# A diffusion-transformer layer on one core: the adaLN vectors move from VectorE to TensorE, and the sums of the projection from GpSimd to VectorE

## Chip, cores and metric

The kernel runs on one core of a Trainium2 chip. The metric is the device time of one execution in microseconds (us); lower is better. Everything is fp32 at the edges; inputs and weights are read from HBM, the output is written there.

## What is computed

One layer over 1,024 latent tokens of width 1,024, with 256 context tokens. The part that the change touches:

```python
sh1, sc1, gt1, sh2, sc2, gt2 = split(silu(c) @ w_mod + b_mod, 6)   # adaLN; w_mod is 1024 x 6144
h = rmsnorm(x, g_pre1) * (1 + sc1) + sh1
q, k, v, f, g_a, g_f = split(h @ w_in)                             # the projection
... attention, Fourier mixing, gated merge, w_out ...
x = x + gt1 * rmsnorm(y, g_post1)
h2 = rmsnorm(x, g_pre2) * (1 + sc2) + sh2
x = x + gt2 * rmsnorm(conv_ffn(h2), g_post2)
```

`sh1` and `sc1` are needed before the first projection matmul. `gt1`, `sh2`, `sc2` and `gt2` are needed only after the merge, far behind the projection.

## The kernel before

**Products.** A fp32 product is three fp32r matmuls (`mm3`, L83 to L87): high part by high, high by low, low by high. Each operand is split by `split`: a copy on ScalarE gives the high part (`hP_g`, `T2a0`), a subtraction on VectorE (L68) the low part (`lP_g`, `T2a1`).

**Items.** The projection is a Strassen product (Winograd's form, function `wino`). Thirteen pairs of 128-column blocks of `w_in` (`g0` to `g7` for the gates, `kv`, `q0`, `q2`, `f0`, `f2`) have seven products each, `P1` to `P7`: 91 items. An item is 12 matmuls of 128x512 into one PSUM bank `X`, `Y` or `Z`. The weights' side needs four sums of two inputs for each pair, `S1` to `S4` (`do_add`; tiles `S_g`, `A_g`); in the kernel before GpSimd makes them. The activations' side is made once: `B11`, `B21`, `B22` and the sums `T1` to `T4n`, cut from the tiles `hr` (`hraw`), which are the normed, transposed and modulated tokens.

**Norm stage.** The first 17 items (0 to 16: `P1`, `P2`, `P5`, `P6`, `P7` of `g0` to `g2`, then `P4` and `P3` of `g0`) are mixed with the loading, squaring, scaling, turning (`turn`, `ptx`) and modulating of the tokens, in an order written out by hand under `tc.manual_schedule()`. An engine takes its instructions in just that order. The first two adaLN vectors are made there on TensorE: `mod_rows` multiplies 32-column groups of the vector (`sv32`) with stages of `w_mod` (`ws`, tiles of the pool `ha`), `mod_copy`, `mod_turn` and `mod_vec` bring the result into columns.

**Projection.** Items 17 to 90 run in `run(17, NI - 5)` and a few lines behind it. For each item `lead` prepares what comes some items later; hooks set by `at(k)` run ahead of item k. The eight other adaLN groups (512 columns each) are made by such hooks: `adaln_load` loads 128x512 pieces of `w_mod` into `wm` tiles (six buffers), `adaln_step` adds one piece, times an element of the vector, to a running sum on VectorE (L723, L725), and `gate_rows` or `col_vec` sums over partitions with a matmul of ones (`pg`, L686, and `pc`, L699). `gate_rows` also loads two rows (`bt`, `gp`), combines them with the result and stores it for later. Behind the projection come the key, value and context pieces and the attention.

**Queues.** All DMAs named here are issued by SP in program order, and each waits for the one eight places ahead of it to land.

Of the kernel before, what the change touches and what calls it, by code (L numbers as in the profile page):

```python
# [16 lines left out]
P = 128  # L17
# [23 lines left out]
def block_kernel(ctx: ExitStack, tc: tile.TileContext, t: dict, out: bass.AP, dbg: dict):  # L41
# [28 lines left out]
    def add(out, a, b, eng=None):  # L70
        return tt(out, a, b, ALU.add, eng)

    def sub(out, a, b, eng=None):
        return tt(out, a, b, ALU.subtract, eng)
# [130 lines left out]
                    items.append((j, p))  # L205
        return items

    def wino(pairs, items, psf, hooks, slots=False):

        st = [dict() for _ in pairs]

        def ready(j):

# [25 lines left out]
        def do_add(j, o):  # L241

            d, nm, w = st[j], pairs[j][2], pairs[j][4] * P
            if o in d:
                return
            if o == "S1":
                d[o] = s(f"{o}_{nm}")[:, :w]
                add(d[o], d["A21"], d["A22"], nc.gpsimd)
            elif o == "S3":
                d[o] = d["A21"]  # L250
                sub(d[o], d["A11"], d["A21"], nc.gpsimd)
            elif o == "S2":
                d[o] = d["A11"]
                sub(d[o], d["S1"], d["A11"], nc.gpsimd)
            else:
                d[o] = d["A12"]
                sub(d[o], d["A12"], d["S2"], nc.gpsimd)

        def do_conv(j, p, eng=None):
            if p in st[j]:  # L260
# [417 lines left out]
    def at(k, *fns):  # L678
        hooks.setdefault(k, []).extend(fns)
# [1 line left out]


    def gate_rows(i, h):
        def done(acc):
            pg = ps(f"pg{i}{h}")
            nc.tensor.matmul(pg, ones, acc, start=True, stop=True)  # L686
            bt, gp = s(f"bt{i}{h}"), s(f"gp{i}{h}")
            load(out=bt, in_=t["rows"][2 * i:2 * i + 1, h * 512:(h + 1) * 512].to_broadcast([P, 512]))
            load(out=gp, in_=t["rows"][2 * i + 1:2 * i + 2, h * 512:(h + 1) * 512].to_broadcast([P, 512]))
            add(bt, pg, bt)  # L690
            mul(bt, bt, gp, nc.gpsimd)
            store(out=gt_d[i, :, h * 512:(h + 1) * 512], in_=bt)
        return done

    def col_vec(w, h):
        def done(acc):
            pc = ps(f"pc{w}{h}")
            for k in range(4):
                nc.tensor.matmul(pc[:, k:k + 1], acc[:, k * P:(k + 1) * P], ones[:, 0:1], start=True, stop=True)  # L699
# [9 lines left out]
    groups = []  # L709
    for h in range(2):  # L710
        for c0, done in ((2 * D, gate_rows(0, h)), (3 * D, col_vec(0, h)), (4 * D, col_vec(1, h)), (5 * D, gate_rows(1, h))):
            groups.append((c0 + h * 512, done))
    wmt, accs = {}, {}

    def adaln_load(i):
        g, k = divmod(i, KT)
        wmt[i] = wm_load(k, groups[g][0])

    def adaln_step(i):
        g, k = divmod(i, KT)  # L720
# [6 lines left out]
    def a0(i):  # L727
        return 17 + i * 7 // 8

    for i in range(8 * KT):  # L730
        at(a0(i), lambda i=i: adaln_load(i))
        at(a0(i) + 4, lambda i=i: adaln_step(i))
        if i % KT == KT - 1:
            at(a0(i) + 7, lambda g=i // KT: groups[g][1](accs[g]))
# [106 lines left out]
    c128, alt = [], []  # L841
    for i, k in enumerate((14, 11)):
        at(NI - k, lambda i=i: late_loads(i))
    run, lead, main, pre, conv, sums, mm, evac, after, st = wino(pairs, items, ps, hooks)
    with tc.manual_schedule():
        for tk in range(4):
            x_load(tk)
# [41 lines left out]
        mod_copy(0)  # L889
        mod_turn(0)  # L890
        mod_vec(0)
        for c in (0, 1, 2, 3):
            x_first(c, (0, 1))
        hb_part(hb, "B11", {c: hraw[c, 0] for c in (0, 2, 1, 3)}, 0, 2)
        mod_rows(1, range(8))
        mod_copy(1)
        mod_turn(1)
        mod_vec(1)
        for tk in range(4):
            x_first(tk, (2, 3))  # L900
# [28 lines left out]
        engs = (nc.vector, None, nc.gpsimd, nc.vector)
        b21 = {c: hraw[c, 1] for c in (0, 3, 1, 2)}  # L930
        for c in range(4):
            x_second(c, (0, 1), engs[c])
        mod_vec(3)
        hb_part(hb, "B21", b21, 0, 2, nc.gpsimd)
# [12 lines left out]
        conv(1, "P2")
        x_square(7)
        x_norm(6)
        for tk in (6, 7):  # L950
            x_scale(tk, 0, nc.vector)
        hb_part(hb, "B21", b21, 2, 4)
        for tk in (4, 5):
            x_scale(tk, 1, nc.gpsimd)
        conv(2, "P2")
        mm(4, range(2))
        for tk in (4, 5):
            x_first(tk, range(4))
        mm(3, range(2, 4))
# [11 lines left out]
        for tk in (6, 7):
            x_scale(tk, 1, nc.gpsimd)
        hb_puts(hb, "T1", {c: hraw[c, 0] for c in range(2)})
        t1(2)
        t1(3)
        conv(0, "P5")
        hb_puts(hb, "T1", {c: hraw[c, 0] for c in range(2, 4)})
        for j in range(1, 3):
            sums(j, "S1")
        for j in range(3):  # L980
            evac(j)
        for j in range(3, 6):
            evac(j, True)
        for tk in (4, 5):
            x_first(tk, range(4), 1)
        conv(1, "P5")
        mm(6)
        for tk in (6, 7):
            turn(tk, 1)
        conv(2, "P5")  # L990
        for j in range(7, 9):
            mm(j)
# [10 lines left out]
        for j in range(9, 12):
            mm(j)
        for c in range(4):
            sub(hraw[c + 4, 0], hraw[c + 4, 1], hraw[c + 4, 0], nc.gpsimd)
# [12 lines left out]
        for j in range(12, 15):
            mm(j)  # L1020
# [1040 lines left out]
```

## Time and profile before

| | |
|---|---|
| median of 3 runs | 1392.88 us (1390.83 to 1396.58) |
| profiled execution | 1390.7 us |
| its span, first to last instruction | 1388.9 us, mean granted clock 0.972 |
| TensorE, VectorE, ScalarE, GpSimd busy | 92%, 77%, 49%, 46% of the span |

The profiled execution is 2.2 us under the median, and 1.8 us of it lie outside the span. A matmul's busy time overlaps its neighbour's, so the pace of TensorE is read from the starts of its matmuls, and its idle time from the waits. The granted clock is a share of full speed: 1.00 is 2.4 GHz, 0.50 is 1.2 GHz.

### The profile page before, as it was taken

The numbers are of one execution on the slowest core, as the hardware profiler recorded it, in microseconds if no ns is written. First come the engines' busy times: TensorE is split into PE (matmuls) and PEld (weight loads), VectorE is DVE, ScalarE is ACT, GpSimd is POOL, SyncE is SP. The second block draws the span as 40 slices with busy tenths as digits, with TensorE's granted clock in tenths as the row PEclk, the third lists the DMA queues.
The fourth block names the chain that finished last, engine by engine and source line by source line (L and its number), as shares of the span: only waits on it lengthen the run. The fifth ranks groups of instructions, "written<-read, shape, count | busy, mean of one in ns | idle before, by whom it ended". The sixth has DMA issues, their size and how long they took to land.

```text
span 1388.9 us, 18347 instructions
## 1 busy us (share of the span) xinstructions
PE 1275.4 (92%) x5848; PEld 1031.8 (74%) x5848; DVE 1075.3 (77%) x1714; ACT 676.2 (49%) x1392; POOL 632.1 (46%) x471
## 2 busy tenths in 40 slices
PE   4759989998999999999979999999999988989896
PEld 3548878776878877777757788888888876878774
DVE  4587899988688986644899997666666687796977
ACT  5456334235567675323756554444444454443442
POOL 0483556553243333611586444444344345372754
PEclk9879999999999999999999999999999999999998
DMA  9714766753524344813603465444434559846563
GB/s 306 228 43 131 238 207 229 251 143 116 142 69 134 110 124 122 302 59 106 190 16 99 131 174 143 129 128 111 121 107 126 167 163 290 294 137 223 180 205 122
DMA packets 251125, 219.42 MB, mean 158 GB/s; under 512 B 14972, under 2 KB 204052, under 8 KB 251028
## 3 DMA queue, kind: packets, MB, share of 16 engines
q1 hardware_dynamic: 251028, 218.25, 51.1%
q8 instruction: 46, 0.75, 0.2%
q14 instruction: 51, 0.42, 0.1%
HBM read 159.20 MB, written 58.72 MB: 157 GB/s over the span
## 4 chain that ended last, share of the span: by engine, by line
PE 52%; DVE 23%; DMA 9%; issue 7%; ACT 4%; POOL 3%; SPq 1%; DVEq 0%; POOLq 0%; ACTq 0%
PE X_u L86 5%; PE X_u L87 5%; PE X_u L85 5%; PE Y_u L85 2%; PE Y_u L87 2%; PE Y_u L86 2%; DVE p L1219 2%; DVE pl L68 2%; PE X_d L85 2%; PE X_d L86 2%; PE X_d L87 2%; DMA ws<-in_w_mod 2%; DVE lP_g L68 1%; PE y L85 1%; PE Z_u L86 1%
## 5 line engine op out<-in xcount | busy, mean ns | idle before, releaser
L68 DVE TENSOR_TENSOR lP_u<-A_u,hP_u 128x512 fp32r<-128x512 f32 x132 | 103.8, 795 | 45.5 <-ACT hP_u L299 45.5
L361 ACT COPY snP_u<-X_u 128x512 f32<-128x512 f32 x57 | 33.5, 587 | 140.8 <-PE X_u L87 132.5
L68 POOL TENSOR_TENSOR A_u<-A_u,A_u 128x512 f32<-128x512 f32 x44 | 71.5, 1625 | 36.4 <-DVE lP_u L68 18.2
L1239 POOL TENSOR_SCALAR p<-p,sm 128x640 f32<-128x640 f32 (+1 forms) x64 | 48.3, 775 | 84.3 <-PE pp L1244 39.2
L68 POOL TENSOR_TENSOR yd<-yd,snP_d 128x512 f32<-128x512 f32 x36 | 52.0, 1448 | 72.8 <-ACT snP_d L361 72.8
L68 POOL TENSOR_TENSOR A_u<-S_u,A_u 128x512 f32<-128x512 f32 x22 | 29.5, 1343 | 107.3 <-DVE lP_u L68 107.0
L299 ACT CAST hP_u<-A_u 128x512 fp32r<-128x512 f32 x121 | 74.6, 619 | 0.1
L361 ACT COPY snP_d<-X_d 128x512 f32<-128x512 f32 x48 | 28.1, 585 | 83.2 <-PE X_d L87 81.6
L80 ACT CAST ph<-pp 128x512 fp32r<-128x512 f32 x76 | 44.3, 585 | 23.3 <-PE pp L1244 21.9
L68 DVE TENSOR_TENSOR pl<-pp,ph 128x512 fp32r<-128x512 f32 x76 | 51.7, 681 | 3.2 <-ACT ph L80 2.7
L1233 ACT ACTIVATE p<-p,nm 128x640 f32<-128x640 f32 (+1 forms) x64 | 51.3, 802 | 0.7 <-DVE nm L1226 0.7
L1549 POOL TENSOR_SCALAR z<-xr,ry 128x512 f32<-128x512 f32 x15 | 16.7, 1123 | 75.3 <-DVE ry L68 65.1
L68 DVE TENSOR_TENSOR lP_d<-rP_d,hP_d 128x384 fp32r<-128x384 f32 x48 | 42.3, 882 | 10.8 <-ACT hP_d L299 10.5
L1244 PE MATMUL pp<-ident,p 128*128 128x128 f32 x304 | 47.0, 274 | 3.9 <-DVE pl L68 2.0
L1219 DVE CUSTOM_DVE_ANT_0 p<-ss,mask 128x640 f32<-128x640 f32 (+1 forms) x64 | 49.9, 782 | 0.0
L725 DVE SCALAR_TENSOR_TENSOR acc<-wm,sv,acc 128x512 f32<-128x512 f32 x56 | 49.2, 879 | 0.6
L1244 PEld LDWEIGHTS pp<-ident,p 128*128 128x128 f32 x304 | 37.0, 140 | 13.6 <-POOL p L1239 3.7
L68 POOL TENSOR_TENSOR wd<-wd,wd 128x512 f32<-128x512 f32 x22 | 37.0, 1700 | 20.3 <-DVE dB L68 11.5
L1624 DVE SCALAR_TENSOR_TENSOR tb<-u,vec,tb 128x1024 f32<-128x1024 f32 x22 | 40.2, 1827 | 6.9 <-ACT tb L1621 6.9
L68 DVE TENSOR_TENSOR u<-Y_u,snP_u 128x512 f32<-128x512 f32 x22 | 15.2, 690 | 38.7 <-PE Y_u L87 38.7
L68 DVE TENSOR_TENSOR dB<-wd,dB 128x512 fp32r<-128x512 f32 x33 | 38.8, 1185 | 8.1 <-ACT dB L1695 8.0
L68 DVE TENSOR_TENSOR lP_g<-A_g,hP_g 128x512 fp32r<-128x512 f32 x48 | 40.3, 853 | 4.5 <-ACT hP_g L80 4.4
(893 smaller groups left out, 4719.9 us busy)
## 6 DMA issues: line engine op xcount, KB each, us to landing
A_u<-in_w_up SPq DMA_DIRECT2D x88, 256.0 KB, 3.7
wm<-in_w_mod SPq DMA_DIRECT2D x66, 256.0 KB, 5.3
wd<-in_w_down SPq DMA_DIRECT2D x55, 256.0 KB, 4.1
A_g<-in_w_in SPq DMA_DIRECT2D x32, 256.0 KB, 5.3
ws<-in_w_mod SPq DMA_DIRECT2D x30, 256.0 KB, 6.0
bP_d<-g_d0P SPq DMA_DIRECT2D x56, 128.0 KB, 3.2
x<-in_x SPq DMA_DIRECT2D x16, 256.0 KB, 5.6
sga_d<-c_g SPq DMA_DIRECT2D x16, 256.0 KB, 3.0
```

Source lines behind the costliest of these rows:

```text
L68: return (eng or nc.vector).tensor_tensor(out=out, in0=a, in1=b, op=op)
L80: copy(hi, src)
L85: nc.tensor.matmul(ps, ah, bh, start=start, stop=False, skip_group_check=True)
L86: nc.tensor.matmul(ps, ah, bl, start=False, stop=False, skip_group_check=True)
L87: nc.tensor.matmul(ps, al, bh, start=False, stop=stop, skip_group_check=True)
L299: copy(st[j]["half", p][0], st[j][STA[p]])
L361: copy(d["s" + p], d["X"])
L725: nc.vector.scalar_tensor_tensor(out=accs[g], in0=wmt[i], scalar=sv[:, k:k + 1], in1=accs[g], op0=ALU.mult, op1=ALU.add)
L1219: nc.vector.tensor_tensor_reduce(out=p_, in0=ssc[:, lo:768], in1=self.mk, op0=ALU.add, op1=ALU.max, scale=1.0, scalar=-3.0e38, accum_out=s ...
L1233: nc.scalar.activation(out=self.pt[g], in_=self.pt[g], func=AF.Exp, scale=SCALE, bias=self.m[:, g:g + 1], accum_out=self.sm[:, g:g + 1])
L1239: nc.gpsimd.tensor_scalar(out=self.pt[g], in0=self.pt[g], scalar1=self.sm[:, g:g + 1], scalar2=1.0, op0=ALU.mult, op1=ALU.mult)
L1244: nc.tensor.transpose(pp[:, g * P:(g + 1) * P], self.pt[g][:, j * P:(j + 1) * P], ident)
```

## The change

Three things change together.

1. The eight adaLN groups go to TensorE in 32-column groups, as `mod_rows` does already. `ada_load` loads the eight pieces of a group, `ada_rows` multiplies them in two halves of four matmuls, `ada_copy` copies the bank out on ScalarE, and `ada_done` calls `gate_rows` or `col_vec`, which now use `sel0` and `sel` in place of `ones`. Groups 0 to 5 (both halves of gate 1, shift 2, scale 2) stand in the norm stage's hand order, 0 and 1 with `gate_rows`, 2 to 5 with `col_vec`; groups 6 and 7 (gate 2) are hooks of items 20 to 45.
2. The sums `S1` to `S4` of the projection, the product `bt * gp`, and the two-input and scaling work of the norm stage leave GpSimd for VectorE (the second scalings `x_scale(tk, 1, ...)` and part of `x_second` for ScalarE).
3. The norm stage's hand order is new: whole items in place of halves, `x_second` and `B21` earlier, `T1` in one piece, sums and conversions of `P5` and `P6` item by item.

```diff
-    def wino(pairs, items, psf, hooks, slots=False):
+    def wino(pairs, items, psf, hooks, slots=False, seng=None):
+        seng = seng or nc.gpsimd
-                add(d[o], d["A21"], d["A22"], nc.gpsimd)
+                add(d[o], d["A21"], d["A22"], seng)
...
     def gate_rows(i, h):
-        def done(acc):
+        def done(rows):
             pg = ps(f"pg{i}{h}")
-            nc.tensor.matmul(pg, ones, acc, start=True, stop=True)
+            nc.tensor.matmul(pg, sel0, rows, start=True, stop=True)
             bt, gp = s(f"bt{i}{h}"), s(f"gp{i}{h}")
...
             add(bt, pg, bt)
-            mul(bt, bt, gp, nc.gpsimd)
+            mul(bt, bt, gp)
...
-    def adaln_step(i):
-        g, k = divmod(i, KT)
-        if k == 0:
-            accs[g] = s(f"acc{g}")
-            nc.vector.tensor_scalar_mul(accs[g], wmt[i], sv[:, k:k + 1])
-        else:
-            nc.vector.scalar_tensor_tensor(out=accs[g], in0=wmt[i], scalar=sv[:, k:k + 1], in1=accs[g], op0=ALU.mult, op1=ALU.add)
...
+    def ada_load(g, ks, spare=True):
+
+        for k in ks:
+            if k < 6 and spare:
+                if k % 3 == 0:
+                    st_.append(hbp.tile([P, 3, 512], F, tag="ha", name=f"wa{g}{k}", bufs=10))
+                wmt[g, k] = st_[-1][:, k % 3, :]
+                load(out=wmt[g, k], in_=w_mod[k * P:(k + 1) * P, groups[g][0]:groups[g][0] + 512])
+            else:
+                wmt[g, k] = wm_load(k, groups[g][0])
+
+    def ada_rows(g, half):
+        if half == 0:
+            rowp[g] = ps(f"ar{g}")
+        for k in range(half * 4, half * 4 + 4):
+            o = k % 4 * 32
+            nc.tensor.matmul(rowp[g][o:o + 32, :], sv32[:, k, :], wmt[g, k], start=k < 4, stop=k >= 4, skip_group_check=True)
+
+    def ada_copy(g):
+        rows = s(f"ac{g}")
+        copy(rows, rowp[g])
+        rowp[g] = rows
+
+    def ada_done(g):
+        groups[g][1](rowp[g])
+
+
+    for g in (6, 7):
+        k0 = 20 + (g - 6) * 10
+        for k in range(KT):
+            at(k0 + k, lambda g=g, k=k: ada_load(g, (k,), False))
+        at(k0 + 8, lambda g=g: ada_rows(g, 0))
+        at(k0 + 12, lambda g=g: (ada_rows(g, 1), ada_copy(g)))
+        at(k0 + 15, lambda g=g: ada_done(g))
...
-    run, lead, main, pre, conv, sums, mm, evac, after, st = wino(pairs, items, ps, hooks)
+    run, lead, main, pre, conv, sums, mm, evac, after, st = wino(pairs, items, ps, hooks, seng=nc.vector)
...
+        ada_load(4, range(KT))
         for tk in (4, 5):
             turn(tk, 1)
...
+        ada_done(0)
         mm(6)
         for tk in (6, 7):
             turn(tk, 1)
+        sums(2, "S1")
         conv(2, "P5")
...
+        mm(7)
+        ada_rows(2, 0)
         for j in range(3):
             sums(j, "S3")
             sums(j, "S2")
+        conv(0, "P6")
+        mm(8)
+        ada_rows(2, 1)
+        ada_done(1)
         for c in range(4):
             sub(hraw[c, 0], hraw[c + 4, 1], hraw[c, 0])
...
         hb_puts(hb, "T2", {c: hraw[c, 0] for c in range(4)})
...
+        mm(12)
+        ada_rows(5, 1)
+        ada_copy(5)
+        mm(13)
+        mm(14)
+        ada_done(5)
         hb_puts(hb, "T4n", {c: hraw[c, 0] for c in range(4)})
         hb_puts(hb, "B22", {c: hraw[c + 4, 1] for c in range(4)})
```

**SP's queue behind the rope tables.** In the kernel before, six pieces of adaLN (`wm2048`) follow the rope tables, and then nothing until the first stores of the norm stage (`sga`).

```order
L599 DMA rope10_125<-in_rope 128x512
L599 DMA rope11_126<-in_rope 128x512
L463 DMA wm2048_0_1113<-in_w_mod 128x512
L463 DMA wm2048_1_1115<-in_w_mod 128x512
L463 DMA wm2048_2_1138<-in_w_mod 128x512
L463 DMA wm2048_3_1160<-in_w_mod 128x512
L463 DMA wm2048_4_1183<-in_w_mod 128x512
L463 DMA wm2048_5_1207<-in_w_mod 128x512
L647 DMA sga_d_78<-c11_g0_748 128x512
L647 DMA sga_d_78<-c11_g1_750 128x512
```

In the changed kernel 40 loads of 256 KB follow the rope tables at that place, those of groups 0 to 4 (`wa` with three pieces to a tile, and `wm`); the end of these is shown. Then come `bt00` and `gp00` for `gate_rows(0, 0)`.

```order
L464 DMA wm3584_6_781<-in_w_mod 128x512
L464 DMA wm3584_7_783<-in_w_mod 128x512
L725 DMA wa40_800<-in_w_mod 128x512 x3
L725 DMA wa43_804<-in_w_mod 128x512 x3
L464 DMA wm4096_6_808<-in_w_mod 128x512
L464 DMA wm4096_7_810<-in_w_mod 128x512
L692 DMA bt00_852<-in_rows 128x512
L693 DMA gp00_853<-in_rows 128x512
L696 DMA gt_d_82<-bt00_852 128x512
L692 DMA bt01_946<-in_rows 128x512
```

What moved: the two row loads of the first gate group went from the projection into the norm stage, behind the loads of five groups.

**VectorE ahead of items 7 to 9.** In the kernel before, behind the three outputs `c11` of the first items, stand the modulation of a token tile, the low parts of `P5` for items 7 and 8, another token tile and the `T2` sums.

```order
L68 TENSOR_TENSOR c11_g2_752<-Z_g2_691,snP1_g2_746 128x512
L541 TENSOR_SCALAR hr41_754<-ptx41_704,ax_69,sx_70 128x128 x4
L68 TENSOR_TENSOR lP5_g1_765<-S1_g1_738,hP5_g1_764 128x512
L68 TENSOR_TENSOR lP5_g2_792<-S1_g2_740,hP5_g2_791 128x512
L541 TENSOR_SCALAR hr61_821<-ptx61_781,ax_69,sx_70 128x128 x4
L68 TENSOR_TENSOR hr00_368<-hr41_754,hr00_368 128x512
```

In the changed kernel the sum with `bt00` and the product with `gp00` stand between the low part for item 7 and the sum and low part for item 8.

```order
L68 TENSOR_TENSOR c11_g2_832<-Z_g2_728,snP1_g2_826 128x512
L68 TENSOR_TENSOR S1_g1_834<-A21_g1_226,A22_g1_228 128x512
L68 TENSOR_TENSOR lP5_g1_837<-S1_g1_834,hP5_g1_836 128x512
L68 TENSOR_TENSOR bt00_852<-pg00_850,bt00_852 128x512
L68 TENSOR_TENSOR bt00_852<-bt00_852,gp00_853 128x512
L68 TENSOR_TENSOR S1_g2_882<-A21_g2_230,A22_g2_232 128x512
L68 TENSOR_TENSOR lP5_g2_885<-S1_g2_882,hP5_g2_884 128x512
L68 TENSOR_TENSOR A21_g0_222<-A11_g0_172,A21_g0_222 128x512
```

What moved: VectorE now passes a sum that reads a loaded row and the bank `pg00` before it makes anything for item 8 or for `T2`. TensorE's item 7 takes the bank that `pg00` leaves, and so stands behind the same sum.

**VectorE at the last item before the projection's `run`.** In the kernel before, the low parts of `P7` are followed at once by those of `T4n`.

```order
L68 TENSOR_TENSOR lP7_g0_937<-A21_g0_220,hP7_g0_936 128x512
L68 TENSOR_TENSOR lP7_g1_941<-A21_g1_224,hP7_g1_940 128x512
L68 TENSOR_TENSOR lP7_g2_945<-A21_g2_228,hP7_g2_944 128x512
L68 TENSOR_TENSOR T4na1_249<-hr00_368,T4na0_248 128x3x128
L68 TENSOR_TENSOR T4na1_249<-hr10_371,T4na0_248 128x3x128
```

In the changed kernel two short instructions that read `pc11` stand ahead of them (`hr` are the `T4n` sums, made by GpSimd before).

```order
L68 TENSOR_TENSOR lP7_g2_1116<-A21_g2_230,hP7_g2_1115 128x512
L68 TENSOR_TENSOR hr00_370<-hr01_325,hr00_370 128x512
L68 TENSOR_TENSOR hr10_373<-hr11_327,hr10_373 128x512
L68 TENSOR_TENSOR hr20_376<-hr21_349,hr20_376 128x512
L68 TENSOR_TENSOR hr30_379<-hr31_351,hr30_379 128x512
L68 TENSOR_TENSOR a2_71<-pc11_1177,vec_67 128x4
L709 SCALAR_TENSOR_TENSOR a2_71<-a2_71,vec_67 128x4
L68 TENSOR_TENSOR T4na1_251<-hr00_370,T4na0_250 128x3x128
L68 TENSOR_TENSOR T4na1_251<-hr10_373,T4na0_250 128x3x128
```

What moved: on TensorE `pc11` stands behind item 14, and `T4n` is read by item 15, so all of `T4n` and `B22` on VectorE now lies between the two items.

## Rows read from the trace of the kernel before

**Rows 1.** Part 1 of the page, TensorE: busy us (share of the span), instructions.

```profile
PE 1275.4 (92%) x5848; PEld 1031.8 (74%) x5848; DVE 1075.3 (77%) x1714; ACT 676.2 (49%) x1392; POOL 632.1 (46%) x471
```

**Rows 2.** Stretches: length, busy us (instructions) of each engine, granted clock, DMA share, GB/s.

```profile
26.00:97.00 71.00, 45.05 (x200) 32.68 (x201) 53.86 (x122) 35.74 (x97) 37.44 (x31) 0.78 0.51 163
97.00:120.00 23.00, 22.66 (x94) 18.30 (x93) 16.45 (x35) 17.10 (x43) 7.33 (x6) 0.94 0.27 82
120.00:180.00 60.00, 60.00 (x268) 49.44 (x267) 50.50 (x65) 21.91 (x42) 31.39 (x21) 1.00 0.65 209
180.00:240.00 60.00, 56.53 (x236) 45.29 (x235) 55.31 (x72) 23.24 (x44) 32.02 (x20) 0.94 0.71 232
240.00:300.00 60.00, 56.20 (x251) 45.15 (x250) 59.44 (x92) 20.56 (x38) 34.60 (x23) 1.00 0.62 195
300.00:357.00 57.00, 51.36 (x249) 42.13 (x248) 39.99 (x91) 28.82 (x58) 19.86 (x16) 0.97 0.52 150
```

**Rows 3.** Waits of TensorE, 122 to 357 us: us in total, times, longest.

```profile
PE X_g L87 <- DVE lP_g L68: 5.3, 3, 3.0
PE ptc L157 <- DVE cx L748: 4.3, 2, 3.8
```

**Rows 4.** Timeline of TensorE at items 6 and 17: start, us, work.

```profile
77.79 0.80 PE L85 MATMUL Y_g<-T1a,hP_g 128*128 128x512 f32 x1 [8.63 <-DVE c_g L68]
...
78.81 0.63 PE L87 MATMUL Y_g<-T1a,lP_g 128*128 128x512 f32 x1
79.23 0.63 PE L85 MATMUL Y_g<-T1a,hP_g 128*128 128x512 f32 x1
...
83.69 0.48 PE L85 MATMUL Y_g<-T1a,hP_g 128*128 128x512 f32 x1
...
120.02 0.39 PE L85 MATMUL X_g<-T4na,hP_g 128*128 128x512 f32 x1
120.25 0.39 PE L86 MATMUL X_g<-T4na,hP_g 128*128 128x512 f32 x1
```

**Rows 5.** The norm stage's loads on SP's queue: first issue, time to issue all.

```profile
47.88 2.25 SPq L599 DMA_DIRECT2D rope<-in_rope  x4
50.18 3.94 SPq L463 DMA_DIRECT2D wm<-in_w_mod  x6
94.42 1.67 SPq L647 DMA_DIRECT2D sga_d<-c_g  x3
```

**Rows 6.** Groups of TensorE, 120 to 357 us.

```profile
L699 PE MATMUL pc<-ones,acc 128*128 128x1 f32 x32 | 4.3, 247 | 0.0
L686 PE MATMUL pg<-acc,ones 128*128 128x512 f32 x8 | 4.1, 592 | 0.0
```

**Rows 7.** Timeline of TensorE around an adaLN product of the norm stage.

```profile
38.38 1.92 PE L570 MATMUL mr<-ws,sv 128*32 128x512 f32 x16
40.24 0.50 PE L85 MATMUL X_g<-B11a,hP_g 128*128 128x512 f32 x1
```

**Rows 8.** Groups of VectorE, 122 to 330 us: busy us, mean ns, idle before.

```profile
L725 DVE SCALAR_TENSOR_TENSOR acc<-wm,sv,acc 128x512 f32<-128x512 f32 x56 | 49.2, 879 | 0.6
L68 DVE TENSOR_TENSOR lP_g<-A_g,hP_g 128x512 fp32r<-128x512 f32 x26 | 24.7, 954 | 2.0 <-ACT hP_g L80 1.9
```

**Rows 9.** Timeline of VectorE, 84 to 115 us.

```profile
84.90 6.22 DVE L68 TENSOR_TENSOR hr<-hr,hr 128x512 f32<-128x512 f32 x4
...
93.92 1.95 DVE L68 TENSOR_TENSOR T2a<-hr,T2a 128x384 fp32r<-128x384 f32 x4
95.79 0.89 DVE L68 TENSOR_TENSOR T2b<-hr,T2b 128x128 fp32r<-128x128 f32 x4
...
114.77 0.68 DVE L68 TENSOR_TENSOR c_g<-Y_g,snP_g 128x512 f32<-128x512 f32 x1
```

**Rows 10.** Groups of GpSimd, 122 to 330 us.

```profile
L68 POOL TENSOR_TENSOR A_g<-A_g,A_g 128x512 f32<-128x512 f32 x10 | 15.4, 1540 | 3.4 <-issue 2.3 <-POOL fo L68 0.8
```

**Rows 11.** DMA issues, 0 to 130 us: KB each, median us to landing.

```profile
wm<-in_w_mod SPq DMA_DIRECT2D x8, 256.0 KB, 5.6
```

More of the change, by code (lines that the diff above doesn't have):

```diff
@@ L695, in col_vec, with done @@
     def col_vec(w, h):
-        def done(acc):
+        def done(rows):
             pc = ps(f"pc{w}{h}")
             for k in range(4):
-                nc.tensor.matmul(pc[:, k:k + 1], acc[:, k * P:(k + 1) * P], ones[:, 0:1], start=True, stop=True)
+                nc.tensor.matmul(pc[:, k:k + 1], rows[:, k * P:(k + 1) * P], sel[:, 0:1], start=True, stop=True)
             ks = slice(h * 4, h * 4 + 4)
@@ L727, in a0 @@
[L727 to L734, printed above, removed]
+    groups = [((c0 * 2 + h) * 512, done) for c0, f in ((2, lambda h: gate_rows(0, h)), (3, lambda h: col_vec(0, h)),
+                                                       (4, lambda h: col_vec(1, h)), (5, lambda h: gate_rows(1, h)))
+              for h, done in ((h, f(h)) for h in range(2))]
@@ L891, in block_kernel, with alt_ @@
         mod_vec(0)
-        for c in (0, 1, 2, 3):
-            x_first(c, (0, 1))
+        def alt_(i):
+            return nc.vector if i % 2 else None
+        for c in range(4):
+            x_first(c, (0, 1), 0, alt_(c))
         hb_part(hb, "B11", {c: hraw[c, 0] for c in (0, 2, 1, 3)}, 0, 2)
         mod_rows(1, range(8))
+        ada_load(0, range(KT))
+        conv(0, "P1")
+        mm(0, range(2))
         mod_copy(1)
+        conv(1, "P1")
         mod_turn(1)
@@ L916, in block_kernel @@
         mod_rows(3, range(4, 8))
+        ada_load(2, range(KT))
+        hb_part(hb, "B21", b21, 0, 2)
+        conv(0, "P2")
         mod_copy(3)
         mod_turn(3)
+        x_square(4)
+        x_square(5)
+        mod_vec(3)
         def turn(tk, kh):
@@ L927, in t1 @@
             sub(hraw[c, 0], hraw[c + 4, 0], hraw[c, 0], eng)
[L929 to L934, printed above, removed]
         for c in range(4):
             x_second(c, (2, 3), engs[c])
-        x_square(4)
-        x_square(5)
-        conv(0, "P2")
+        hb_part(hb, "B21", b21, 2, 4)
+        mm(3)
         x_norm(4)
@@ L951, in block_kernel @@
             x_scale(tk, 0, nc.vector)
-        hb_part(hb, "B21", b21, 2, 4)
         for tk in (4, 5):
[L954 to L959, printed above, removed]
+            x_first(tk, range(4), 0, alt_(tk))
+        ada_rows(0, 0)
         for tk in (6, 7):
             turn(tk, 0)
-        mm(4, range(2, 4))
-        t1(0, nc.gpsimd)
-        t1(1, nc.gpsimd)
-        sums(0, "S1")
-        for tk in (6, 7):
-            x_first(tk, range(4))
-        mm(5)
+        for tk in (6, 7):
+            x_first(tk, range(4), 0, alt_(tk))
+        mm(5)
+        ada_rows(0, 1)
+        for c in range(4):
+            t1(c)
+        sums(0, "S1")
+        hb_puts(hb, "T1", {c: hraw[c, 0] for c in range(4)})
+        conv(0, "P5")
+        ada_copy(0)
+        ada_load(3, range(KT))
+        for tk in range(4, 8):
+            x_scale(tk, 1, None)
+        ada_rows(1, 0)
+        ada_rows(1, 1)
+        ada_copy(1)
+        ada_load(4, range(KT))
         for tk in (4, 5):
             turn(tk, 1)
[L971 to L979, printed above, removed]
         for j in range(3):
@@ L997, in block_kernel @@
             sums(j, "S2")
+        conv(0, "P6")
+        mm(8)
+        ada_rows(2, 1)
+        ada_done(1)
         for c in range(4):
             sub(hraw[c, 0], hraw[c + 4, 1], hraw[c, 0])
-        for j in range(3):
-            conv(j, "P6")
         hb_puts(hb, "T2", {c: hraw[c, 0] for c in range(4)})
[L1003 to L1006, printed above, removed]
+        ada_copy(2)
+        ada_load(5, range(KT))
+        ada_rows(3, 0)
+        ada_rows(3, 1)
+        ada_done(2)
+        ada_copy(3)
+        conv(1, "P6")
+        conv(2, "P6")
+        mm(9)
+        ada_rows(4, 0)
+        ada_done(3)
         for j in range(4, 7):
@@ L1009, in block_kernel @@
         evac(9)
+        for c in range(4):
+            sub(hraw[c + 4, 0], hraw[c + 4, 1], hraw[c + 4, 0])
+        mm(10)
+        ada_rows(4, 1)
+        ada_copy(4)
         hb_puts(hb, "T3", {c: hraw[c + 4, 0] for c in range(4)})
+        mm(11)
+        ada_rows(5, 0)
+        ada_done(4)
         for j in range(3):
```

57 lines of the change are left out of this document (26 added, 31 removed).

## Prediction

> **What bounds the kernel now.** I read part 1 of the page first: TensorE is busy 92% of the span [rows 1]. A gain can only come from its idle 8%, from stretches at a lower granted clock, or from matmuls that are no longer issued. The order of instructions on every engine is the same in both kernels behind the projection's last item, so I looked at the first 357 us alone, by stretches [rows 2].
>
> In the norm stage, 26 to 97 us, TensorE works 45.05 of 71 us at a mean granted clock of 0.78: something else sets the pace. In the projection, 120 to 357 us, TensorE is busy 60.00 + 56.53 + 56.20 + 51.36 = 224.1 of 237 us, so 12.9 us are idle. VectorE is busy 50.50 + 55.31 + 59.44 + 39.99 = 205.2 us, and 59.44 of 60 between 240 and 300. TensorE's waits in that stretch say why: the largest are for a low part `lP_g` (5.3 us) and for the context tokens `cx` (4.3 us), both made by VectorE [rows 3]. So the projection is a nearly full TensorE whose gaps are VectorE's lateness.
>
> Two more places matter. In the timeline, item 6 starts at 77.79 after a wait of 8.63 us, and its matmuls then start 0.42 us apart (78.81, 79.23). At 120.02, where the hand order is over and item 17 starts, they are 0.23 us apart [rows 4]: 1.2 against 2.4 GHz. An item of 12 takes 12 x 0.23 = 2.76 us at the full clock, 5.0 at half. And SP issues the rope tables and six adaLN pieces from 47.88 to 54.1 us and then nothing until 94.42 [rows 5].
>
> **The projection.** *Removed from TensorE:* the adaLN sums over partitions, 4.3 us (`pc`) and 4.1 us (`pg`) [rows 6]. Half of `pg` stays, 2.05 us. *Added there:* two groups of eight 32-column products. Eight such products of the norm stage take the place from 38.38 to 40.24, 1.86 us [rows 7], so 3.7 us. Net 8.4 - 2.05 - 3.7 = 2.6 us less.
>
> *VectorE:* the 56 accumulations go, 49.2 us at 0.879 each [rows 8], and eight first products of about 0.68, together 54 us. Added are four sums for each of ten pairs. The two bounds for one are 0.68 us, a two-input piece of that size with GpSimd idle, and 6.22 / 4 = 1.55 us, such a piece beside a busy GpSimd [rows 9]. I take 0.68, since it is GpSimd that loses these sums, 1.54 us each [rows 10], some 62 us: 40 x 0.68 = 27 us. The low parts run beside less of that work. They take 0.954 us now [rows 8], and 0.68 alone; over some 55 low parts in the projection that is up to 15 us less. VectorE's load becomes 205 - 54 + 27 - 15 = 163 us in a projection of about 220. With the dear price for a sum and no relief it is 213, which still fits but just so.
>
> With 57 us of slack on VectorE, I let the 12.9 us of gaps fall to 4. Part remains since `cx` and the first low parts behind a load are late for other reasons than load on VectorE. The granted clock of 0.94 and 0.97 in two stretches [rows 2] costs 0.06 x 60 + 0.03 x 57 = 5.3 us; I let it go with the gaps. Sum for the projection: -2.6 - 8.9 - 5.3 = **-16.8 us**. Bounds: -20.8 with no gap left, -12 if half of gaps and clock loss stay.
>
> The sums themselves are where a rule of the notes bears. The Trainium skill (Perfetto Trace Analysis, Optimizing Scalar/DVE Operations) says that GpSimd and VectorE share a read port of SBUF, so that moving operations between the two might not help. The rows here put 27 us of new sums against up to 15 us of relief, so the move alone costs VectorE some 12 us, and what frees it is the accumulations; by the rule taken strictly the move would be neutral, and the load 151 instead of 163. Either leaves TensorE the bound.
>
> **The norm stage, first stop: a row on SP's queue.** The 40 loads of groups 0 to 4 are issued where six stood, from 50.18 us. Each waits for the one eight places ahead, and a load lands 5.6 us after its issue when the queue is full [rows 11]: 5.6 / 8 = 0.70 us a load. The lower bound is the ten loads of [rows 5], 6.24 / 10 = 0.62. So `bt00` is issued at 50.2 + 28 = 78.2 and lands at 83.8; VectorE's sum is done at D = 84.5. With 0.62 it is 81; if one load has to wait for its buffer, a landing more, 90. VectorE is there far earlier, since its pieces that take 1.55 beside GpSimd now take 0.68: by my estimate at 72 to 73. It stands for some 11 us, and with it, queued behind on VectorE, the sum and low part for item 8, all of `S2` to `S4` and `T2`. TensorE stands too, since item 7 needs the bank of `pg00`. The lead that the new order gains ahead of this point (eight to ten us by the same estimate) is lost whole. In the kernel before, item 7 starts at 83.69 [rows 4]; now it starts at 84.6. Groups 0 and 1 on TensorE (four halves, 3.7 us) are hidden by the 26 us of idle TensorE in that stage; without that cover they cost 3.7.
>
> **The norm stage, from item 7 on.** In the kernel before, items 7 to 16 take 120.0 - 83.7 = 36.3 us. Now there stand on TensorE, one behind the other:
> - ten items at 2.76 us: 27.6 us.
> - groups 2 to 5, eight halves at 0.93: 7.4 us.
> - `pg01` at 1.0 (4.1 us / 4) and four `pc` groups at 1.07 (4.3 / 4) [rows 6]: 5.3 us. Idle TensorE no longer covers these, since there is little left in 97 to 120 us, 22.66 of 23 busy [rows 2].
> - a stop ahead of item 9. Behind `pg01` VectorE has two gate pieces and four `T2` sums (6 x 0.68) and the `T2a` low parts (1.95) [rows 9] to do, 6.0 us; TensorE has group 3 and `pc00`, 2.9. It waits 3.1 us.
> - a second stop at item 15. VectorE takes `pc11` ahead of `T4n` and `B22`, and `pc11` stands behind item 14. Behind it VectorE needs 1.95 + 0.89 for `T4n` and as much again for `B22` [rows 9], then 0.68 for the low part: 6.4 us, and two matmuls, 0.5 us, lie beside it. Item 12 waits in the same way for two short instructions behind `pc10` and one low part, less two matmuls: about 0.5. Together 6.4 us.
> - the half clock behind each of the three long stops: a dozen matmuls at 0.42 in place of 0.23 would be 2.3 us, as at 77.79; I take 2 each, 6 us.
>
> Sum 55.8, so item 17 starts at 84.6 + 55.8 = 140.4 instead of 120.0: **+20.4 us**. Bounds +14 (D at 81, stops half as long) and +26 (D at 90).
>
> **The sum.** +20.4 - 16.8 = +3.6 us. On the profiled execution, 1390.7 us (its span and 1.8 us around it), that gives 1394.3; the median of the runs shown is 2.2 us above it, so I expect 1396.5, rounded to 1397 us. About half a per cent, 7 us, is what a measurement can tell from no change.
>
> **Rivals.**
> *Faster, the lead is kept* (chance 0.2). If `bt00` came before VectorE asks for it, item 7 would start near 73.5, 11 us earlier: +9.4 - 16.8 = -7.4, or 1386; with a projection at its best bound 1382. Against it: `bt00` would have to be issued by 67 us, 40 loads in 17 us, 0.42 us each, while nothing in the rows is issued faster than 0.56 [rows 5]. The same time comes if the two later stops are half as long and the projection reaches its best bound, +14 - 20.8 = -7. That is the likelier way.
>
> *Slower, the projection isn't freed* (0.25). The sums stood on GpSimd, where a wait for a late piece of `w_in` held nobody else. On VectorE the same wait holds all low parts behind it. It decides once such waits pass the slack of 57 us over ten pairs, 5.7 us a pair, one landing [rows 11]. Then the gaps stay and only the 2.6 us of TensorE's work and some of the clock are won, say 5 us: +20.4 - 5 = +15, 1408 us. For it: `lP_g` waits are already the first cause [rows 3]. Against: the loads stand many items ahead of their use.
>
> *No difference, the new products keep the clock up* (0.1). The groups of products fill the idle time that lowers the clock in the norm stage, and the half clock of 6 us behind the stops doesn't come: 1391 us. Against: all three stops lie where TensorE has no product ready. The Trainium skill (TensorE: Matmul & The Clock Gate, Part 1) says that the clock follows how busy the engine has been of late; the trace agrees, with steps of 0.42 us after the wait of 8.63 [rows 4].
>
> **How the numbers follow.** The forecast case, both stops there and the projection freed, has 0.4 and spans 1391 to 1402. With the rivals' 0.2, 0.25 and 0.1, and 0.05 for what I don't see, the range of 8 in 10 is 1382 to 1410. Faster than 1386: the faster half of the first rival and a little more, 0.17. Slower than 1400: the slower rival and the upper part of the forecast, 0.37. Between, 0.46.
>
> **What will show it.** In the changed kernel's profile: SP issues `w_mod` pieces without a break from 50 to about 78 us; VectorE waits for a DMA (`bt`) for some 11 us until about 84, and TensorE's item 7 waits for VectorE's `bt`; TensorE's item 15 waits about 6 us for `T4na` and `lP_g`; item 17 starts near 140; from there to the start of the attention's first products 220 instead of 237 us, with VectorE near 75% busy. The prediction is wrong if `bt00` lands before 75 us, if the 16 items' end lies under 130 or over 147 us, or if the projection stays over 228 us.

## The result, and the profile after

The changed kernel takes 1398.4 us (median of 11 runs, 1397.06 to 1401.75), the kernel before 1392.0 us in the same comparison. The ratio is 1.005, with a 95% interval from 1.0036 to 1.0064: 6.4 us slower. The forecast was 1397.

Part 1 of the page answers to [rows 1]: TensorE is busier, VectorE and GpSimd are less so, and the span has grown from 1388.9 to 1398.8 us.

```profile
PE 1298.2 (93%) x5976; PEld 1037.7 (74%) x5976; DVE 1029.7 (74%) x1713; ACT 687.2 (49%) x1416; POOL 519.8 (37%) x393
```

The stretches, with the same columns as [rows 2]: length, busy us of each engine, granted clock, DMA share, GB/s. The hand order ends near 143 us here, the projection near 368.5.

```profile
26.00:97.00 71.00, 55.53 (x248) 35.17 (x248) 41.20 (x120) 36.98 (x102) 0.00 (x0) 0.83 0.88 298
97.00:120.00 23.00, 19.40 (x105) 12.04 (x106) 15.32 (x37) 13.95 (x31) 0.00 (x0) 0.93 0.72 226
120.00:143.00 23.00, 17.57 (x72) 12.93 (x71) 14.83 (x33) 12.53 (x31) 0.00 (x0) 0.85 0.26 79
143.00:203.00 60.00, 60.00 (x267) 46.03 (x266) 39.96 (x59) 23.16 (x43) 12.30 (x8) 1.00 0.52 165
203.00:263.00 60.00, 60.00 (x264) 47.43 (x263) 40.44 (x59) 24.88 (x46) 12.64 (x8) 1.00 0.45 140
263.00:323.00 60.00, 60.00 (x267) 49.67 (x266) 46.57 (x90) 22.31 (x43) 16.67 (x12) 1.00 0.45 132
323.00:368.50 45.50, 41.34 (x204) 34.70 (x203) 32.60 (x77) 25.40 (x51) 9.24 (x8) 0.92 0.43 130
```

In the first row TensorE does 55.5 us of work where it did 45.1, at a higher granted clock: the norm stage is filled as was meant. From 143 us on TensorE is never idle for 180 us, where it lost 3.5 and 3.8 us in two of three such stretches, and VectorE works 40 to 47 of 60 us in place of 50 to 59. Both gains are plain, and the kernel is slower. What was lost lies ahead of 143 us: a wait of 7.0 us in the first row, shown below, and 97 to 143 us, where TensorE works 37.0 of 46 us.

The timeline of SP's queue (first issue, time to issue all) shows 40 adaLN pieces behind one another and the first gate row after them:

```profile
51.04 4.29 SPq L725 DMA_DIRECT2D wa<-in_w_mod  x6
...
77.79 1.01 SPq L464 DMA_DIRECT2D wm<-in_w_mod  x2
79.15 0.33 SPq L692 DMA_DIRECT2D bt<-in_rows  x1
79.82 0.33 SPq L693 DMA_DIRECT2D gp<-in_rows  x1
86.02 0.33 SPq L696 DMA_DIRECT2D gt_d<-bt  x1
```

Waits of VectorE, 40 to 145 us (us in total, times, longest), with the row first:

```profile
DVE bt L68 <- DMA bt<-in_rows: 9.4, 1, 9.4
DVE a L68 <- PE pc L703: 7.6, 2, 6.6
```

Waits of TensorE, 25 to 145 us:

```profile
PE Y_g L85 <- DVE bt L68: 7.0, 1, 7.0
PE X_g L87 <- DVE lP_g L68: 4.1, 2, 3.6
PE pc L703 <- ACT ac L738: 3.0, 1, 3.0
...
PE X_g L86 <- DVE T4na L68: 1.6, 1, 1.6
```

The timeline of TensorE, with item 7, then `pc11` and item 15, then item 17, and last the first product behind the projection, `pab` (start, us, work, [wait]):

```profile
85.32 0.80 PE L85 MATMUL Y_g<-T1a,hP_g 128*128 128x512 f32 x1 [7.01 <-DVE bt L68]
85.91 0.63 PE L86 MATMUL Y_g<-T1a,hP_g 128*128 128x512 f32 x1
86.33 0.63 PE L87 MATMUL Y_g<-T1a,lP_g 128*128 128x512 f32 x1
...
128.52 0.94 PE L703 MATMUL pc<-sel,ac 128*128 128x1 f32 x8
129.66 0.50 PE L85 MATMUL X_g<-T4na,hP_g 128*128 128x512 f32 x1 [0.20 <-ACT snP_g L290]
131.80 0.49 PE L86 MATMUL X_g<-T4na,hP_g 128*128 128x512 f32 x1 [1.64 <-DVE T4na L68]
135.90 0.80 PE L87 MATMUL X_g<-T4na,lP_g 128*128 128x512 f32 x1 [3.60 <-DVE lP_g L68]
136.49 0.63 PE L85 MATMUL X_g<-T4na,hP_g 128*128 128x512 f32 x1
136.92 0.63 PE L86 MATMUL X_g<-T4na,hP_g 128*128 128x512 f32 x1
...
143.30 0.39 PE L85 MATMUL X_g<-T4na,hP_g 128*128 128x512 f32 x1
...
368.47 1.95 PE L1191 MATMUL pab<-c,fd 128*128 128x128 f32 x16
```

The same product in the kernel before:

```profile
356.95 1.95 PE L1145 MATMUL pab<-c,fd 128*128 128x128 f32 x16
```

`bt00` is issued at 79.15, VectorE stands for 9.4 us, and TensorE for 7.0 us behind it; then the matmuls start 0.42 us apart. Item 7, which started at 83.69 before [rows 4], starts at 85.32. The second stop is item 15: VectorE stood for 6.6 us (the longer of its two waits for `pc`) until TensorE, at 128.52, reached `pc11`. Item 15's second matmul waits 1.64 us for `T4na`, its third 3.60 us for the low part at the end of VectorE's queue, and what follows runs at 1.2 GHz again. Item 17 starts at 143.30, against 120.02 in [rows 4].

So the norm stage costs 23.3 us more. The first product behind the projection starts at 368.47 instead of 356.95: the projection takes 225.2 us where it took 236.9, 11.8 less. The balance at that point is +11.5, and the span's +9.9 follows, since the rest of the program is 1.6 us shorter in this execution. That rest lies between 1028.0 and 1032.0 us in all ten profiles of this document, so the 1.6 us need no cause of their own.

### The profile page after: what moved, and what is told of

Same layout as the page of the kernel before. It is cut to its first block, busy times and chain, and to the rows that moved or that the text cites. A ratio compares the mean times of both kernels' runs of the same rounds, so it can differ in the third digit from the quotient of the medians.

```text
span 1398.8 us, 18469 instructions
## 1 busy us (share of the span) xinstructions
PE 1298.2 (93%) x5976; PEld 1037.7 (74%) x5976; DVE 1029.7 (74%) x1713; ACT 687.2 (49%) x1416; POOL 519.8 (37%) x393
## 5 line engine op out<-in xcount | busy, mean ns | idle before, releaser
L68 POOL TENSOR_TENSOR shk<-shk,rope 128x512 f32<-128x512 f32 x2 | 3.2, 1604 | 163.8 <-ACT c_g L618 157.3
L68 POOL TENSOR_TENSOR wd<-wd,wd 128x512 f32<-128x512 f32 x22 | 37.0, 1702 | 20.5 <-DVE dB L68 11.5
L68 POOL TENSOR_TENSOR S_u<-A_u,A_u 128x512 f32<-128x512 f32 x22 | 39.1, 1781 | 8.0 <-PE X_u L86 7.5
```

The source lines that it names most:

```text
L68: return (eng or nc.vector).tensor_tensor(out=out, in0=a, in1=b, op=op)
```

## The experiments

All times are medians; the runs of the kernel before that go with them have medians of 1390.97 us (for the row, the small sum and the two runs on the sums) and 1390.73 us (for the other four). On that ground the changed kernel, 1.005 of before, stands at 1397 to 1398.

Theory A: the changes cost time in the norm stage through two stops that the order makes (a row behind 40 loads on SP's queue, a small sum ahead of two big splits on VectorE) and through TensorE work that no idle time covers; the projection gains since the accumulations leave VectorE. Rival B: the traffic of 12.6 MB holds the norm stage back. Rival C: TensorE's extra products alone are the loss. A last rival has the sums, not the accumulations, as what frees the projection.

**The row ahead of the loads.** `bt00` and `gp00` are issued 16 loads earlier.

```diff
+        gate_load(0, 0)
         ada_load(3, range(KT))
...
+    btgp = {}
+
+    def gate_load(i, h):
+        bt, gp = btgp[i, h] = s(f"bt{i}{h}"), s(f"gp{i}{h}")
+        load(out=bt, in_=t["rows"][2 * i:2 * i + 1, h * 512:(h + 1) * 512].to_broadcast([P, 512]))
+        load(out=gp, in_=t["rows"][2 * i + 1:2 * i + 2, h * 512:(h + 1) * 512].to_broadcast([P, 512]))
...
     def gate_rows(i, h):
         def done(rows):
             pg = ps(f"pg{i}{h}")
             nc.tensor.matmul(pg, sel0, rows, start=True, stop=True)
-            bt, gp = s(f"bt{i}{h}"), s(f"gp{i}{h}")
-            load(out=bt, in_=t["rows"][2 * i:2 * i + 1, h * 512:(h + 1) * 512].to_broadcast([P, 512]))
-            load(out=gp, in_=t["rows"][2 * i + 1:2 * i + 2, h * 512:(h + 1) * 512].to_broadcast([P, 512]))
+            if (i, h) not in btgp:
+                gate_load(i, h)
+            bt, gp = btgp[i, h]
```

> The changed kernel with one edit: the two row loads of the first gate group (bt00, gp00) are issued ahead of the loads of group 3 instead of behind those of group 4, 16 loads earlier. Theory A (the lead is lost by the place on SP's queue): the row lands near 74 instead of 84.5 us, VectorE's 9.4 us wait goes, item 7 starts near 76 instead of 85.3, and the time falls by 8 to 10 us against the changed kernel, to about 1389. Rival B (the stream of 12.6 MB itself holds the stage back, by its traffic): the wait only moves to another load or another engine, under 3 us of gain. Rival C (TensorE's extra products alone are the loss): item 7 starts earlier, but item 17 still starts at about 143.

1388.36 us, ratio to before 0.9984 (0.9972 to 0.9995): some 9 us faster than the changed kernel. VectorE no longer waits for the row; the timeline has the sum at 74.26 instead of 84.57, right behind the low part ahead of it:

```profile
73.65 0.69 DVE L68 TENSOR_TENSOR lP_g<-S_g,hP_g 128x512 fp32r<-128x512 f32 x1 [0.74 <-ACT hP_g L80]
74.26 0.68 DVE L68 TENSOR_TENSOR bt<-pg,bt 128x512 f32<-128x512 f32 x1
74.98 0.69 DVE L68 TENSOR_TENSOR bt<-bt,gp 128x512 f32<-128x512 f32 x1
```

Item 7 starts at 77.32 instead of 85.32, and item 17 at 135.16, 8.1 us earlier. The same bytes cross the same queue, so rival B falls as the cause of this loss; TensorE does the same products, so rival C can't be the whole.

**The small sum behind the splits.** `pc11` and its two VectorE instructions stand behind items 15 and 16.

```diff
-        ada_done(5)
         hb_puts(hb, "T4n", {c: hraw[c, 0] for c in range(4)})
         hb_puts(hb, "B22", {c: hraw[c + 4, 1] for c in range(4)})
...
         for k in range(15, 17):
             lead(k)
             mm(k)
             evac(k)
+        ada_done(5)
```

> The changed kernel with one edit: the call that makes pc11 and its two short VectorE instructions stands behind items 15 and 16 instead of ahead of the T4n and B22 splits. Theory A: VectorE makes T4n and B22 during items 12 to 14, TensorE's waits of 1.6 and 3.6 us at item 15 and the half clock behind them (some 2 us) go, and the time falls by 6 to 8 us against the changed kernel, to about 1391. Rival: T4n's high parts on ScalarE or the sums ahead of them are late too, then under 3 us.

1390.6 us, ratio to before 1.0 (0.999 to 1.0011): 7 us faster than the changed kernel. In the timeline of TensorE item 15 starts after a wait for ScalarE's copy of its bank and then runs on at once, at the full clock:

```profile
127.65 0.50 PE L85 MATMUL X_g<-T4na,hP_g 128*128 128x512 f32 x1 [1.02 <-ACT snP_g L290]
127.99 0.40 PE L86 MATMUL X_g<-T4na,hP_g 128*128 128x512 f32 x1
128.25 0.50 PE L87 MATMUL X_g<-T4na,lP_g 128*128 128x512 f32 x1
128.58 0.40 PE L85 MATMUL X_g<-T4na,hP_g 128*128 128x512 f32 x1
```

**Both edits.**

> The changed kernel with both edits: bt00 and gp00 ahead of the loads of group 3, and pc11 behind items 15 and 16. Theory A (the two stops stand one behind the other on TensorE's path, and the projection's gain is untouched): the gains add up, some 17 us below the changed kernel, 1380 to 1383, 8 to 11 us below the kernel before. Rival (with the first stop gone a later one takes its place, so that the gains overlap): 1386 to 1390.

1382.03 us, ratio to before 0.9942 (0.9925 to 0.9959). That is some 15 us below the changed kernel, of 9 and 7 us for the edits alone. The two gains add up but for about 1 us: the stops stood one behind the other on TensorE's path, and the kernel is now faster than before.

**And `T2` ahead of the second gate group.** The prediction's third stop, at item 9, was left. The profile after has it as a wait of `pc` for ScalarE's copy `ac` (3.0 us): on ScalarE that copy stands behind the high parts of `T2`, and these wait for sums that stand behind `bt01` on VectorE.

```diff
-        ada_done(1)
+        ada_copy(2)
         for c in range(4):
             sub(hraw[c, 0], hraw[c + 4, 1], hraw[c, 0])
         hb_puts(hb, "T2", {c: hraw[c, 0] for c in range(4)})
-        ada_copy(2)
+        ada_done(1)
```

> Both edits of the run before, and a third: T2 and the copy of group 2 stand ahead of the second gate group (pg01, bt01) on VectorE and ScalarE instead of behind it. Theory A: VectorE's wait of 3.1 us for pg01 no longer holds T2, ScalarE's copy of group 2 no longer stands behind T2's high parts, TensorE's wait of 3.0 us ahead of item 9 and its half clock go: 3 to 5 us below the run with both edits, 1376 to 1379. Rival (T2 then waits for something else, a token tile): under 1.5 us.

1375.76 us, ratio to before 0.9894 (0.9876 to 0.9912): 6.3 us below the run with both edits, more than the 3 to 5 forecast. The edit moves two things at once, the copy ahead of `T2` on ScalarE and `T2` ahead of the gate group on VectorE; which of them would do alone wasn't tried. The wait for the copy is 0.8 us in the waits of TensorE (60 to 120 us):

```profile
PE pc L710 <- ACT ac L745: 0.8, 1, 0.8
```

That is 2.2 us less. Item 9 runs at the full clock and takes 2.9 us instead of 5.3 from its first start to the next work's, a wait of 0.8 us ahead of group 3 is gone, and `pc00` is 0.8 us shorter: some 6 us, where the forecast had counted the wait and the half clock alone. Item 17 starts at 119.23, against 143.30 in the changed kernel and 120.02 before:

```profile
119.23 0.49 PE L85 MATMUL X_g<-T4na,hP_g 128*128 128x512 f32 x1
```

**The sums alone, on the kernel before.** For the ten later pairs `S1` to `S4` go to VectorE; the accumulations stay there too.

```diff
+            eng = seng if seng and j >= 3 else nc.gpsimd
-                add(d[o], d["A21"], d["A22"], nc.gpsimd)
+                add(d[o], d["A21"], d["A22"], eng)
```

> The kernel before with one part of the change alone: the sums S1 to S4 of the ten later pairs on VectorE; the adaLN accumulations stay on VectorE, the norm stage stays as it was. Theory A (the accumulations, not the sums, are what held the projection): VectorE gets 27 us of sums and loses up to 15 us of slowdown beside GpSimd, it is busy some 215 of 237 us, and the gaps of TensorE grow: no gain, 0 to 10 us slower, 1392 to 1402. Rival (taking the sums off GpSimd is what frees the projection): 5 us faster or more, 1387 or less.

1389.86 us, ratio 0.9989 (0.9979 to 0.9999): a thousandth faster, where 0 to 10 us slower were forecast. The stretches answer to [rows 2] row by row:

```profile
120.00:180.00 60.00, 60.00 (x268) 49.40 (x267) 50.87 (x76) 23.26 (x43) 13.85 (x9) 1.00 0.62 200
180.00:240.00 60.00, 56.31 (x239) 44.61 (x238) 55.94 (x84) 22.47 (x42) 15.93 (x9) 0.97 0.70 234
240.00:300.00 60.00, 56.73 (x250) 46.36 (x249) 57.01 (x103) 19.32 (x36) 17.94 (x13) 0.97 0.60 190
300.00:357.00 57.00, 50.48 (x243) 40.75 (x242) 39.61 (x92) 29.04 (x58) 10.93 (x9) 0.97 0.54 152
```

VectorE is busy 203.4 us in these stretches, with 37 of the 40 sums in them, against 205.2. What it does beside the sums has become about as much shorter as the sums are long: the low parts `lP_f` take 0.864 us each instead of 1.176 (groups of VectorE, 120 to 357 us, before and in this run: busy us, mean ns, idle before).

```profile
L68 DVE TENSOR_TENSOR lP_f<-A_f,hP_f 128x512 fp32r<-128x512 f32 x12 | 14.1, 1176 | 0.0
L68 DVE TENSOR_TENSOR lP_f<-A_f,hP_f 128x512 fp32r<-128x512 f32 x12 | 10.3, 864 | 0.2 <-ACT hP_f L80 0.2
```

TensorE is still idle for 13.5 us, and the projection takes 238.0 us (118.86 to 356.84) against 236.9. So the sums don't free the projection; the loss that was forecast didn't come either, since the load on VectorE stayed where it was and did not rise to 215 us.

**The sums back on GpSimd, in the changed kernel.** The same line the other way round, `eng = seng if j < 3 else nc.gpsimd`.

> The changed kernel with the sums S1 to S4 of the ten later pairs back on GpSimd; all adaLN groups on TensorE. Theory A: VectorE has lost the 54 us of accumulations, its load is about 150 to 165 us either way, and the time is within 3 us of the changed kernel, 1395 to 1401. Rival (the sums are what frees the projection): the projection is 8 us longer or more, 1406 or more.

1399.53 us, ratio to before 1.0064 (1.0048 to 1.0079): 1 to 2 us from the changed kernel. The whole projection in one stretch, with the columns of [rows 2], in this run and in the changed kernel:

```profile
141.07:368.44 227.37, 222.42 (x994) 177.54 (x993) 145.53 (x244) 95.95 (x181) 106.25 (x74) 0.98 0.45 142
143.30:368.47 225.17, 221.01 (x993) 177.58 (x992) 159.27 (x282) 95.46 (x180) 50.86 (x36) 0.98 0.46 142
```

With the sums on GpSimd the projection is 2.2 us longer and TensorE idle for 5.0 us instead of 4.2; little hangs on the sums here either. But VectorE is busy 145.5 us instead of 159.3: without the accumulations beside them the sums do cost VectorE 13.7 us net. That leaves the accumulations as what held the projection, and the last run below shows most of its gaps close when they are moved (with the product `bt * gp`, which goes to VectorE there).

**All adaLN groups in the projection.** The changed kernel without `ada_*` calls in the hand order; the hooks run over all eight groups.

```diff
-    for g in (6, 7):
-        k0 = 20 + (g - 6) * 10
+    for g in range(8):
+        k0 = 17 + g * 15 // 2
...
-        at(k0 + 8, lambda g=g: ada_rows(g, 0))
-        at(k0 + 12, lambda g=g: (ada_rows(g, 1), ada_copy(g)))
-        at(k0 + 15, lambda g=g: ada_done(g))
+        at(k0 + 5, lambda g=g: ada_rows(g, 0))
+        at(k0 + 9, lambda g=g: (ada_rows(g, 1), ada_copy(g)))
+        at(k0 + 12, lambda g=g: ada_done(g))
```

> The changed kernel, but all eight adaLN groups are hooks of the projection, still on TensorE; the norm stage keeps its new hand order without any adaLN work of these groups. Theory A (the norm stage's loss is made of adaLN work and its stops, and TensorE pays about 2.9 us a group with its pc or pg in the projection too): item 17 starts near 110 us, some 33 us earlier, the projection is 17 to 20 us longer, and the time is 1382 to 1388. Rival (the new hand order itself loses time): item 17 starts at 120 or later and the time is over 1393.

1389.19 us, ratio 0.9991 (0.9979 to 1.0003), a little above the range, as the projection became longer than forecast. Item 17 starts at 108.33:

```profile
108.33 0.39 PE L85 MATMUL X_g<-T4na,hP_g 128*128 128x512 f32 x1
```

So the new hand order, with the work that it takes from GpSimd and without these groups, is 11.7 us ahead of the old one, and the six groups with their stops cost 35.0 us in the changed kernel's norm stage (143.30 against 108.33), but 10.9 in the version with three edits (119.23). The projection is 249.0 us long, 23.8 more than with two groups, where 17 to 20 were forecast: about 4 us for each of the six instead of 2.9.

**All adaLN groups on TensorE, on the kernel before.** The same hooks; norm stage and sums as before (`bt * gp` alone goes to VectorE with them).

> The kernel before with one part of the change alone: all eight adaLN groups on TensorE as hooks of the projection; norm stage and sums as before. Theory A: the accumulations leave VectorE and the gaps of 12.9 us shrink to 4 or 5, while TensorE gets eight groups of products, 16 to 23 us, for the 8.4 us of its old adaLN matmuls less those that stay (about 5): about even, 1388 to 1400. Rival (freeing VectorE is worth more than TensorE's products): 1385 or less.

1404.31 us, ratio 1.0103 (1.0085 to 1.012): outside the range, on the slow side. VectorE is freed: it is busy for 150.3 of the 251 us from 120 to 371, and of TensorE's waits over the projection these alone are left,

```profile
PE X_g L87 <- DVE lP_g L68: 5.1, 1, 5.1
PE Z_g L85 <- DVE bt L68: 0.5, 1, 0.5
```

but the products take more of TensorE than that gives back. The group of TensorE instructions, 120 to 371 us (busy us, mean ns, idle before):

```profile
L733 PE MATMUL ar<-wm,sv 128*32 128x512 f32 x128 | 24.3, 605 | 0.0
```

Idle time falls by 7.3 us, from 12.9 to 5.6, and the 128 records of products come as 23 pieces of 1.0 us each, 22.8 us in the starts of their neighbours: +15.5, and the projection is in fact 15.0 us longer (371.30 - 119.35 = 252.0 against 236.9).

## Why the prediction was right, point by point

The forecast was +3.6 us, and the profiled executions are 9.9 apart. Two terms were too small a loss or too large a gain: the norm stage cost 23.3 us and not 20.4, the projection gave 11.8 and not 16.8, together 7.9. Behind the projection 1.6 us came back (3.6 + 7.9 - 1.6 = 9.9). The medians are only 6.4 us apart, as the profiled execution lies 1.3 us under its median before and 2.2 above it after. So the number, 1397 against 1398.4, is nearer than its terms were, and that is luck.

*The row on SP's queue: right.* Forecast: issue at 78.2, sum done at 84.5, item 7 at 84.6. Measured: 79.15, 85.2 and 85.32. VectorE stood for 9.4 us, not 11, since it came there at 75.1 and not at 72 to 73. The first edit shows that the place on the queue, not the traffic, is the cause.

*The stops at items 15 and 9: right in place and size, one cause wrong.* Item 15: 0.20 + 1.64 + 3.60 = 5.4 us, forecast 5.9. Ahead of item 9 TensorE waits 3.0 us, forecast 3.1; but it waits in `pc`, for ScalarE's copy of group 2, and not for VectorE's `T2a`. The step overlooked that ScalarE takes its instructions in order too. The third edit, which moves both, took all but 0.8 us of it away.

*TensorE's own work from item 7 on: slightly low.* From 85.32 to 143.30 are 58.0 us, forecast 55.8. With item 7 0.7 us later than forecast, that is the whole miss of 2.9 us in the norm stage. TensorE's waits in it add up to 9.7 us, forecast 9.5, so what was low is mostly its work; half a group takes 1.0 us there, not 0.93. The lower bound of the term, +14, doesn't come out of its own parts: 3.5 us for D at 81 and 4.75 for stops half as long make it +12.

*VectorE's load in the projection: right.* Forecast 163 us, measured 159.3. The forecast took 27 us of sums against up to 15 of relief, 12 net; with the sums back on GpSimd the load is 145.5, so they cost 13.7 net. Beside the accumulations, in the run with the sums alone, they cancel instead, 203.4 against 205.2 us. So the statement of the Trainium skill (Perfetto Trace Analysis, Optimizing Scalar/DVE Operations), that moving operations between GpSimd and VectorE might not help because they share a read port, agrees with both runs as far as the kernel's time goes. In its strict form, a neutral load, it holds in the run with the accumulations and not in the changed kernel. That the port is the reason is not shown by any of these runs.

*TensorE's gaps in the projection: right.* Forecast 4 us left of 12.9; 4.2 are left. These are TensorE's waits of the changed kernel, 140 to 375 us; the second lies behind the projection:

```profile
PE ptc L157 <- DVE cx L765: 3.8, 1, 3.8
PE pvs L1174 <- DVE abl L68: 0.5, 1, 0.5
PE X_g L85 <- ACT hP_g L80: 0.3, 1, 0.3
```

*TensorE's adaLN work in the projection: the wrong sign.* Forecast 2.6 us less; by the starts of the neighbours it is 1.9 us more. This is 4.5 of the 5.0 us by which the projection missed its forecast. `pc` and `pg` took 5.3 us before, not the 8.4 of their overlapping records; the `pg` that stays takes 1.4; and the products of the two groups, which the scheduler split into five pieces (12, 4, 6, 2 and 8 records), take 5.8, not 3.7. Why five pieces cost so much is in the timeline, where a piece of one matmul (two records) takes as long as one of four (eight records):

```profile
205.91 1.04 PE L734 MATMUL ar<-wm,sv 128*32 128x512 f32 x2
206.88 0.50 PE L85 MATMUL Y_g<-T1a,hP_g 128*128 128x512 f32 x1
...
209.83 1.07 PE L734 MATMUL ar<-wm,sv 128*32 128x512 f32 x8
210.83 0.50 PE L85 MATMUL X_g<-B11a,hP_g 128*128 128x512 f32 x1
```

From 205.91 to 206.88 it is 0.97 us, from 209.83 to 210.83 it is 1.00.

*The clock in the projection: near in size, by something else.* I let 5.3 us go with the gaps, from the granted clock of two stretches. With the waits taken out, the 888 matmuls of the items take 209.9 us from start to start before and 205.0 after, 4.8 less. But only 13 of them ran at half pace in the projection before, behind waits of 3.0 and 3.8 us, and 6 after, behind the one such wait that is left; at 0.2 us each that is 1.4 us. Most of the other 3.4 us lies in single steps of 0.3 to 0.6 us next to a wait or an inserted product, 30 before and 15 after, which the forecast did not have. The granted clock of such a stretch was no measure of matmuls at half pace: it counts waiting too (from 182.8 to 185.8 us before it was 0.88, with TensorE busy for 0.01 us). Gaps -8.8, adaLN work +1.9 and these steps -4.8 make up the 11.8 us but for 0.1.

*The rivals.* The faster one did not come, as `bt00` was issued at 79.15 us and not by 67. The first edit makes its condition true: the row is issued at 67.51, and the kernel takes 1388.4 us, against the 1386 of that rival. The slower one, a projection that isn't freed, did not come. The one in which the products keep the clock up fits what was seen in the stretch with the first stop, where the granted clock was 0.83 against 0.78 (26 to 97 us), though no run shows that the products are the cause; behind the stops the half clock came, as argued (matmuls 0.42 us apart after 85.32 and after 135.90).

## What to carry to other kernels

A small row that an in-order engine needs is as late as the bulk loads ahead of it on its queue (84.57 against 74.26 us for the sum that reads it), so a change that pours loads into an idle stretch has to give every small load and every small consumer behind them a place of its own; three moves of a few lines turned a loss of 6 us into a gain of 15. Work that goes from a nearly full VectorE to a nearly full TensorE is worth the gaps that it closes less the time that it takes there (7.3 against 22.8 us in the last run above). It pays where TensorE stands idle: there six groups cost 10.9 us, in the projection 23.8.

## What the runs showed of the hardware

A piece of 32-column products with 512 columns in fp32 takes about 1.0 us on TensorE at the full clock, whether it has one, two or four matmuls to the four column groups (0.97, 0.98, 1.00 us); eight take 1.86 [rows 7]. Taking 40 two-input sums of 128x512 from GpSimd to VectorE left VectorE's busy time in the projection about as it was while the accumulations ran there too, 203.4 against 205.2 us; without them it rose from 145.5 to 159.3 us.
